# The SSD branch's sample states loaded once and turned on the chip, with the product over them cut into quarters

## The chip, the core and the metric

The kernel runs on one core of one Trainium2 chip. The metric is device time in microseconds of one execution. Five engines work side by side and are tied by semaphores: PE (TensorE, matmuls; its weight loads are listed apart as PEld), DVE (VectorE), ACT (ScalarE), POOL (GpSimd) and SP (SyncE, which here only issues DMA transfers). POOL issues DMA transfers as well.

## What is computed

The program is one inference step of a hybrid decoder layer: a prompt of 256 tokens and 8 sample sequences of 4 tokens go through the same weights. One of its branches is a Mamba-2 state-space scan (SSD) with 32 heads of 64 rows and a state of 128 columns, in 4 groups of 8 heads. For a sample sequence the state `S` comes from memory, and a chunk is its 4 tokens:

```python
    acum = jnp.cumsum(dtc * Ag, axis=1)
    ...
    y = jnp.einsum('bgrij,bjgrp->bigrp', m, xc)
    y = y + jnp.einsum('bign,bgrpn->bigrp', Cc, S) * jnp.exp(acum)[..., None]
    last = acum[:, -1]
    w = jnp.exp(last[:, None] - acum) * dtc
    S = jnp.exp(last)[..., None, None] * S + jnp.einsum('bjgr,bjgn,bjgrp->bgrpn', w, Bc, xc)
```

So each sample state is used twice: it is updated and stored (rows are head and feature, columns the state index n), and it is multiplied with C over n, for which TensorE needs n on the partitions, which is the turned layout. The second term of `y` is called the inter-chunk product below, the first one the own-token product.

## The kernel before

The weights, some 380 MB in float32, stream through SBUF once. A projection (`proj_w`) takes them in tiles of 128x512 elements (two k tiles by 256 columns): SP loads a tile (`raw`, L110, 6 buffers), ACT rounds it to the fast format (`whi`, L103), DVE computes the rest (`wlo`, L105, called the cast below), each with 5 buffers, and PE multiplies: per tile 4 matmuls on line L148, 4 on L149 and 4 on L153, of which the last 4 need the cast. All 288 tokens, prompt and sample, are the 288 moving columns. The scans of one group run inside the projections of the next: a scan is a generator, and `weave` advances it by a step for every so many tiles. After that a scheduler puts every engine's instructions in an order by its own estimate of when each can run; an engine then works strictly in its order and waits where an operand is late.

In `ssd_scan`, once per group, the state work for the samples stands at the end. Before the change, POOL loads each state twice: `load_state` brings it in rows (`sin`, 4 tiles of two sequences, tag `c4` with 6 buffers, 8 transfers of 256 KB a group), and `load_square` brings the same state in 32-column pieces of 128 bytes (`sqr`, tag `e2`, 32 transfers of 64 KB a group, two sequences ahead), so that DVE's transpose of 32x32 blocks (L941) yields the full turned matrix `st`. The updates (`updated`: one matmul on L948 and four DVE operations on L951 for a pair of heads) and the transposes (`turned`) alternate: two transposes, two updates, two transposes, two updates, for each half of the eight sequences. `inter` then does the inter-chunk product (L927: 8 matmuls with a 32-column weight `cdm`, 512 moving columns, four of them side by side in four groups of array columns) and the own-token product (L930). DVE scales and adds (L974, L977), four transposes on PE (L983) bring tokens back to columns, and DVE folds the four column groups (L985).

Of the kernel before, what the change touches and what calls it, by code (L numbers as in the profile page):

```python
# [8 lines left out]
F32 = mybir.dt.float32  # L9
# [20 lines left out]
FF = 5632  # L30
FT = FF // P
BLK = 8
NSQ = 2
RB = 6
WB = 5
STOP = object()
# [6 lines left out]
def hybrid_step(ctx: ExitStack, tc: tile.TileContext, I: dict, O: list):  # L43
# [217 lines left out]
    elcol = p1.tile([P, KT, NB], F32, name="elcol")  # L261
    scst = p1.tile([P, 24, 3 * NB + 3], F32, name="scst")
    rg = p1.tile([P, 4], F32, name="rg")
    cdm = p1.tile([P, NB, NS], F32, name="cdm")
    att = p1.tile([P, 2, P], F32, name="att")
    ats = p1.tile([P, NS], F32, name="ats")
    atsl = p1.tile([P, P], F32R, name="atsl")
    qdm = p1.tile([P, 2, NB, NS], F32, name="qdm")
    for z in (cdm, att, ats, atsl.bitcast(F32), qdm, lr3.bitcast(F32), gw3.bitcast(F32), dtbd, scst):
        G.memset(z, 0.0)  # L270
    acum_d = dram.tile([32, T], F32, name="acum_d")
    ma_d = dram.tile([P, KT, T], F32, name="ma_d")
# [7 lines left out]
    with pool("p0") as p0:  # L280
# [251 lines left out]
        def dt_prep():  # L532
            S.activation(acol, alog, ACT.Exp)
            S.activation(dte, dtx, ACT.Abs)
            S.activation(dte, dte, ACT.Exp, scale=-1.0)
            S.activation(dte, dte, ACT.Ln, bias=1.0)
            yield
            V.scalar_tensor_tensor(dtT, dtx, 0.0, dte, ALU.max, ALU.add)
            V.tensor_scalar(dte, dtT, acol, -1.0, ALU.mult, ALU.mult)
            V.tensor_tensor_scan(acumT, rm_s, dte, 0.0, ALU.mult, ALU.add)  # L540
            nc.sync.dma_start(out=acum_d, in_=acumT)

            srep = p0.tile([32, 2, 4, NS], F32, name="srep")
            V.tensor_copy(srep[:, 0], dtT[:, SEQ:T].unsqueeze(1).to_broadcast([32, 4, NS]))
            V.tensor_copy(srep[:, 1], acumT[:, SEQ:T].unsqueeze(1).to_broadcast([32, 4, NS]))
            sel = p0.tile([P, P], F32, name="sel")
            V.memset(sel, 0.0)
            G.affine_select(sel, sel, pattern=[[0, P]], compare_op=ALU.not_equal, fill=1.0, base=127, channel_multiplier=-1)
            sels = p0.tile([NS, 4, NB, NL], F32, name="sels")
            V.memset(sels, 0.0)  # L550
            G.affine_select(sels, sels, pattern=[[0, 4], [4, NB], [0, NL]], compare_op=ALU.not_equal, fill=1.0, base=3,
                            channel_multiplier=-1)
            elT = p0.tile([32, NB], F32, name="elT")
            S.activation(elT, acumT[:, SEQ:T].rearrange("p (b l) -> p b l", l=NL)[:, :, NL - 1], ACT.Exp)

# [12 lines left out]
            for i in range(3):  # L568
                for w, src in ((0, dtT), (1, acumT)):
                    s_ = src[:, i * P:(i + 1) * P] if i < 2 else srep[:, w].rearrange("p r t -> p (r t)")  # L570
                    TR(a[:, i * 64 + w * 32:i * 64 + w * 32 + 32], s_, ident[0:32, 0:32])
            V.tensor_copy(tokc.rearrange("p c x -> p (c x)"), a[:, 0:192])

            for r in range(4):
                q = slice(r * NS, (r + 1) * NS)
                V.tensor_copy(dtbd[q].rearrange("p (a r) -> p r a", r=4)[:, r],
                              tokc[q, 2, 0:32].rearrange("p (a r) -> p r a", r=4)[:, r])
                V.tensor_copy(acs[q], tokc[q, 2, 32:64].rearrange("p (a r) -> p r a", r=4)[:, r])
            yield
            yield  # L580
            a = mm_tile()
            MM(a[:, 0:32], sel, tokc[:, 0, 32:64], start=True, stop=True)
            MM(a[:, 32:64], sel, tokc[:, 1, 32:64], start=True, stop=True)
            MM(a[:, 64:96], sels.rearrange("p r b l -> p (r b l)"), tokc[0:NS, 2, 32:64], start=True, stop=True)
            V.tensor_tensor(wtok[:, 0:3, :], a[:, 0:96].rearrange("p (c x) -> p c x", x=32), tokc[:, :, 32:64], ALU.subtract)
            V.tensor_copy(wtok[:, 3, :], a[:, 32:64])
            S.activation(wtok, wtok, ACT.Exp)
            S.activation(eas, tokc[:, 2, 32:64], ACT.Exp)
            V.tensor_tensor(wtok[:, 0:3, :], wtok[:, 0:3, :], tokc[:, :, 0:32], ALU.mult)
            V.tensor_tensor(wtok[:, 3, :], wtok[:, 3, :], wtok[:, 0, :], ALU.mult)  # L590
            yield
            a = mm_tile()
            MM(a[:, 0:KT * NB], hsel.rearrange("p e x -> p (e x)"), elm.rearrange("p t b -> p (t b)"), start=True, stop=True)
            V.tensor_copy(elcol.rearrange("p t b -> p (t b)"), a[:, 0:KT * NB])

        weave(mem_proj(I["w_cv"], 2, o_pmv), dt_prep(), KT, 8)
        run(mem_proj(I["w_ck"], 3, o_pmk), mem_proj(I["w_cv"], 3, o_pmv))
# [145 lines left out]
    def ssd_scan(g, xsT, sz):  # L743
# [23 lines left out]
                    in_=I["state_ssd"][2 * q + e, h0:h0 + 8].rearrange("(t e) x n -> (e x) t n", e=2)))  # L767
            sins.append(sin)

        sqs = []  # L770

        def load_square(b):

            sq_ = e2("sqr").rearrange("p a t -> p (a t)")[:, 0:512]
            rows = I["state_ssd"][b, h0:h0 + 8].rearrange("h (y p) (g d) -> g p (h y) d", p=32, d=32)
            for i in range(4):
                tc.keep_in_program_order(G.dma_start(
                    out=sq_[32 * i:32 * i + 32].rearrange("p (r d) -> p r d", d=32), in_=rows[i]))
            sqs.append(sq_)


        bsr = rep4(bT[:, SEQ:T].unsqueeze(1), "bsr")
        yield
        a = mm_tile()
# [62 lines left out]
        for u in range(3):  # L847
# [47 lines left out]
            if u == 1:  # L895
                xsr = rep4(xsT[:, :, SEQ:T], "xsr")
            yield
        for b in range(NSQ):
            load_square(b)
        load_state(0)  # L900
        load_state(1)

        diag(cdm, cT[:, SEQ:T])
        for r in range(2):
            S.activation(mss[:, r, :], mab[:, r, :], ACT.Relu, scale=-1.0, bias=acs[:, 2 * g + r:2 * g + r + 1])
        S.activation(mss, mss, ACT.Exp, scale=-1.0)
# [5 lines left out]
        yield  # L912
        wst = r2("wst")
        stack_l(wst, wxs)
        yield


# [3 lines left out]
        def inter():  # L921
            ysi.append(la_tile())
            ysa.append(mm_tile())
            for q in (1, 0):
                for j in (3, 2, 1, 0):
                    tc.keep_in_program_order(
                        MM(ysi[0][NS * j:NS * j + NS, :], cdm[:, 4 * q + j, :], sts[4 * q + j], start=(q == 1), stop=(q == 0)))  # L927
            for r in range(2):
                tc.keep_in_program_order(
                    MM(ysa[0][NS * r:NS * r + NS, 256 * r:256 * r + 256], mss[:, r, :], xds[:, 256 * r:256 * r + 256],  # L930
                       start=True, stop=True))

        for hf_ in range(2):
            bblk = r2("bblk").rearrange("p (b n) -> p b n", n=P)
# [3 lines left out]

            def turned(b):
                st = b2("st")  # L940
                V.transpose(st, sqs[b])  # L941
                if b + NSQ < NB:
                    load_square(b + NSQ)
                sts.append(st)

            def updated(t):
# [12 lines left out]

            for x in range(4):  # L960
                turned(4 * hf_ + x)
                yield 1.5
                if x % 2 == 0:
                    continue
                for t in ((0, 1) if x == 1 else (2, 3)):
                    updated(t)
                    if hf_ == 0 and t < 2:
                        load_state(2 + t)
                    yield 1.5
        inter()  # L970
        yield
        yield
        ys = b2("ys")
        V.tensor_tensor(heads(ys), heads(ysi[0]), hb(eas[:, h0:h0 + 8], P), ALU.mult)  # L974
        for r in range(2):
            q, c = slice(NS * r, NS * r + NS), slice(256 * r, 256 * r + 256)
            V.tensor_tensor(ys[q, c], ys[q, c], ysa[0][q, c], ALU.add)  # L977
        us = b2("us").rearrange("p (t l) -> p t l", l=P)[:, :, 0:NS]
        V.tensor_tensor(us, xsT[:, :, SEQ:T], dcol[:, 4 * g:4 * g + 4].unsqueeze(2).to_broadcast([P, 4, NS]), ALU.mult)
        yield  # L980
        a = mm_tile()
        for t in range(4):
            TR(a[:, t * P:(t + 1) * P], ys[:, t * P:(t + 1) * P], ident)  # L983
        yt = pa.tile([P, P], F32, tag="cst", bufs=2, name="yt").rearrange("p (t l) -> p t l", l=NS)
        V.tensor_reduce(yt, a.rearrange("p (t j l) -> p t l j", j=4, l=NS), axis=AX.X, op=ALU.add)  # L985
        V.tensor_tensor(us, us, yt, ALU.add)
        V.tensor_tensor(sz[:, :, SEQ:T], us, sz[:, :, SEQ:T], ALU.mult)
        yield

# [997 lines left out]
```

## Time and profile before

| | |
|---|---|
| three runs | 2484.82, 2481.40, 2478.98 us, median 2481.4 |
| profiled execution | 2484.3 us, of which the span of the profile is 2482.6 |
| busy in the span | PE 99%, PEld 96%, DVE 72%, ACT 55%, POOL 18% |
| mean granted TensorE clock | 0.998 |
| DMA | 530.77 MB, mean 214 GB/s |
| the four SSD state stages | the second load of the states begins at 303, 404, 518 and 599 us; the first stage ends at 366, the last at 693 us |

A share of the span is a mean over stages. The idle time that a row gives is that of its engine just before the instruction, with what ended it. A matmul's listed duration includes its way through the pipeline; its pace is the distance between two starts.

### The profile page before, as it was taken

What the parts mean: (1) busy time and instruction counts of PE and PEld (TensorE: products, weight loads), DVE (VectorE), ACT (ScalarE), POOL (GpSimd) and SP (SyncE); (2) the same over time, 40 slices, a digit from 0 to 9 for tenths busy, and PEclk for the clock granted to TensorE, in tenths of its full rate; (3) what the DMA queues carried; (4) which work ended last, traced back from release to release, by engine and by line L of the source; (5) the groups of instructions that cost most, each with busy time, mean ns of one, the idle gap of its engine ahead of it and who ended that gap; (6) DMA issues with size and microseconds to landing.
All of it is one profiled execution on the core that took longest, in us unless ns stands there. A gap on an engine that the chain in (4) does not pass through costs nothing.

```text
span 2482.6 us, 52113 instructions
## 1 busy us (share of the span) xinstructions
PE 2466.2 (99%) x18738; PEld 2388.1 (96%) x18738; DVE 1775.2 (72%) x3804; ACT 1355.8 (55%) x2781; POOL 439.2 (18%) x798
## 2 busy tenths in 40 slices
PE   9999999999999999999999999999999999999998
PEld 8889999999999999999999989999999999999998
DVE  6866778896777766777666577667777676676766
ACT  6766647646464655554455545455555454554545
POOL 3102144143111010110111122402111001020012
PEclk9999999999999999999999999999999999999999
DMA  8877697787768686777778599655555555555555
GB/s 261 263 234 208 165 267 217 208 246 223 223 211 287 207 255 194 240 246 229 224 230 266 182 353 327 196 164 171 170 171 172 171 171 173 170 172 168 170 173 170
DMA packets 457652, 530.77 MB, mean 214 GB/s; under 512 B 40316, under 2 KB 403676, under 8 KB 457360
## 3 DMA queue, kind: packets, MB, share of 16 engines
q1 hardware_dynamic: 420272, 422.39, 56.6%
q0 software_dynamic: 37088, 105.03, 13.2%
q8 instruction: 147, 2.41, 0.4%
q14 instruction: 113, 0.93, 0.1%
q10 hardware_dynamic: 32, 0.01, 0.0%
HBM read 476.41 MB, written 50.86 MB: 212 GB/s over the span
## 4 chain that ended last, share of the span: by engine, by line
PE 96%; DMA 1%; DVE 1%; issue 0%; ACT 0%; SPq 0%; POOL 0%; DVEq 0%; ACTq 0%; POOLq 0%
PE acc L149 28%; PE acc L148 27%; PE acc L153 27%; PE acc L348 2%; PE acc L352 2%; PE acc L349 2%; PE mm L1263 1%; PE la L1254 1%; PE la L1606 1%; DMA kc<-in_cache_mem_k_dram 1%; PE mm L1218 0%; DMA raw<-in_w_ssd_out_dram 0%; PE la L1664 0%; PE la L927 0%; PE mm L948 0%
## 5 line engine op out<-in xcount | busy, mean ns | idle before, releaser
L103 ACT CAST whi<-raw 128x512 fp32r<-128x512 f32 x1464 | 898.1, 618 | 951.5 <-PE acc L149 786.1
L105 DVE TENSOR_TENSOR wlo<-raw,whi 128x512 fp32r<-128x512 f32 x1464 | 995.4, 686 | 534.3 <-ACT whi L103 527.0
L149 PE MATMUL acc<-xn,whi 128*128 128x288 f32 (+1 forms) x1936 | 541.6, 295 | 0.0
L148 PE MATMUL acc<-xn,whi 128*128 128x288 f32 (+1 forms) x1936 | 540.1, 294 | 0.3 <-ACT whi L103 0.3
L153 PE MATMUL acc<-xn,wlo 128*128 128x288 f32 (+1 forms) x1936 | 409.0, 293 | 0.0
L149 PE MATMUL acc<-hf,whi 128*128 128x288 f32 x1408 | 393.3, 296 | 0.0
L148 PE MATMUL acc<-hf,whi 128*128 128x288 f32 x1408 | 388.6, 292 | 0.0
L148 PEld LDWEIGHTS acc<-xn,whi 128*128 128x128 f32 (+1 forms) x1936 | 363.4, 188 | 4.9 <-issue 3.1
L149 PEld LDWEIGHTS acc<-xn,whi 128*128 128x128 f32 (+1 forms) x1936 | 363.7, 188 | 3.6 <-issue 0.4
L153 PEld LDWEIGHTS acc<-xn,wlo 128*128 128x128 f32 (+1 forms) x1936 | 310.4, 188 | 0.8 <-issue 0.4
L153 PE MATMUL acc<-hf,wlo 128*128 128x288 f32 x1408 | 294.5, 290 | 0.0
L149 PEld LDWEIGHTS acc<-hf,whi 128*128 128x128 f32 x1408 | 264.5, 188 | 0.0
L148 PEld LDWEIGHTS acc<-hf,whi 128*128 128x128 f32 x1408 | 264.0, 188 | 0.0
L153 PEld LDWEIGHTS acc<-hf,wlo 128*128 128x128 f32 x1408 | 226.4, 188 | 0.1
L149 PE MATMUL acc<-pr,whi 128*128 128x288 f32 x704 | 196.6, 295 | 0.0
L148 PE MATMUL acc<-pr,whi 128*128 128x288 f32 x704 | 194.8, 293 | 0.0
L1780 POOL COPY fsp<-fst 128x16 f32<-128x16 f32 x88 | 38.5, 440 | 651.8 <-DVE av L1792 433.4
L153 PE MATMUL acc<-pr,wlo 128*128 128x288 f32 x704 | 147.3, 290 | 0.0
L148 PE MATMUL acc<-un,whi 128*128 128x288 f32 x512 | 143.7, 296 | 3.3 <-ACT vT L1044 2.4
L149 PE MATMUL acc<-un,whi 128*128 128x288 f32 x512 | 143.7, 296 | 0.0
L149 PEld LDWEIGHTS acc<-pr,whi 128*128 128x128 f32 x704 | 132.3, 188 | 0.0
L148 PEld LDWEIGHTS acc<-pr,whi 128*128 128x128 f32 x704 | 132.0, 188 | 0.0
(564 smaller groups left out, 4318.4 us busy)
## 6 DMA issues: line engine op xcount, KB each, us to landing
raw<-in_w_in_dram SPq DMA_DIRECT2D x480, 256.0 KB
raw<-in_w_up_dram SPq DMA_DIRECT2D x352, 256.0 KB
raw<-in_w_down_dram SPq DMA_DIRECT2D x176, 256.0 KB
raw<-in_w_ck_dram SPq DMA_DIRECT2D x64, 256.0 KB
raw<-in_w_cv_dram SPq DMA_DIRECT2D x64, 256.0 KB
raw<-in_w_ssd_out_dram SPq DMA_DIRECT2D x64, 256.0 KB
sin<-in_state_gla_dram POOLq DMA_DIRECT2D x32, 512.0 KB, 6.4
out_dram<-sin SPq DMA_DIRECT2D x32, 512.0 KB
```

The costliest lines, as they stand in the source:

```text
L103: S.copy(hi, raw)
L105: V.tensor_tensor(lo, raw, hi, ALU.subtract)
L148: MM(a, hi[:, k, cs], xh, start=(k0 + s0 + k == 0), stop=False)
L149: MM(a, hi[:, k, cs], xl, start=False, stop=False)
L153: MM(a, lo[:, k, cs], xh, start=False, stop=(k0 + s0 + k == nk - 1))
L348: MM(accs[m], mn_hi[:, kk, ms_], hi[:, 0, :], start=(kk == 0), stop=False)
L349: MM(accs[m], mn_lo[:, kk, ms_], hi[:, 0, :], start=False, stop=False)
L352: MM(accs[m], mn_hi[:, kk, ms_], lo[:, 0, :], start=False, stop=(kk == KT - 1))
L1254: MM(osa[NS * j:NS * j + NS, :], qdm[:, k, b, :], sins[b][:, k, :], start=False, stop=(q == 1 and k == 0))
L1263: MM(a, kb[:, k * P:(k + 1) * P], vst, start=True, stop=True)
L1606: MM(ssc[NS * c:NS * c + NS, 0:P], xq[:, j, u, :], kt[:, j], start=(j == 0), stop=(j == 15))
L1780: G.tensor_copy(sp[:, :, 0:2], st.rearrange("p (b k) -> p b k", k=2))
```

## The change

The states are no longer loaded a second time. DVE transposes the rows that `load_state` brought. Because a 32x32 block transpose of rows leaves, in each block of 32 partitions, the state columns of one quarter, the product over n is cut in quarters: a weight `cdx` holds C for one quarter of n in one block of rows and zeros elsewhere, and 32 matmuls with 128 moving columns replace the 8 with 512. Their sums stand by token, block and quarter, and 16 small products with pieces of the identity (a 32-column weight, 32 moving columns) bring them to feature rows. The decays come in a matching layout (`easx`) from two products per program. The own-token product is taken with x as the weight, so that it comes out in feature rows at once. `cdx` is allocated per group in tag `c4` and is zeroed by POOL and filled by 16 small DVE copies. The transposes of a half now stand ahead of all its updates.

```diff
+            esel = p0.tile([NS, 2, P], F32, name="esel")
...
+            for e in range(2):
+                MM(a[:, 0:16], esel[:, e, :], eas[0:NS].rearrange("p (c e) -> p e c", e=2)[:, e], start=(e == 0), stop=(e == 1))
+            V.tensor_copy(easx, a[:, 0:16])
...
-        def load_square(b):
-
-            sq_ = e2("sqr").rearrange("p a t -> p (a t)")[:, 0:512]
-            rows = I["state_ssd"][b, h0:h0 + 8].rearrange("h (y p) (g d) -> g p (h y) d", p=32, d=32)
-            for i in range(4):
-                tc.keep_in_program_order(G.dma_start(
-                    out=sq_[32 * i:32 * i + 32].rearrange("p (r d) -> p r d", d=32), in_=rows[i]))
-            sqs.append(sq_)
...
-        for b in range(NSQ):
-            load_square(b)
         load_state(0)
         load_state(1)
 
-        diag(cdm, cT[:, SEQ:T])
+        cdx = c4([P, NB, 4, NS], "cdx")
+        G.memset(cdx, 0.0)
...
+        for y in range(4):
+            own_ = cdx[32 * y:32 * y + 32].rearrange("p b f (q u l) -> p f u b q l", q=2, u=4)[:, :, y]
+            for f in range(4):
+                base = own_[:, f]
+                V.tensor_copy(
+                    bass.AP(base.tensor, base.offset, [list(base.ap[0]), [4 * P + 16, 2], [P, 4], [1, NL]]),
+                    cT[32 * f:32 * f + 32, SEQ:T].rearrange("p (q j l) -> p q j l", q=2, j=4))
...
             for q in (1, 0):
-                for j in (3, 2, 1, 0):
-                    tc.keep_in_program_order(
-                        MM(ysi[0][NS * j:NS * j + NS, :], cdm[:, 4 * q + j, :], sts[4 * q + j], start=(q == 1), stop=(q == 0)))
-            for r in range(2):
+                for f in range(4):
+                    for j in (3, 2, 1, 0):
+                        b = 4 * q + j
+                        tc.keep_in_program_order(
+                            MM(ysi[0][NS * j:NS * j + NS, 0:P], cdx[:, b, f, :],
+                               sts[b].rearrange("p (t f x) -> p f t x", f=4, x=32)[:, f],
+                               start=(q == 1 and f == 0), stop=(q == 0 and f == 3)))
+            for t in range(4):
                 tc.keep_in_program_order(
-                    MM(ysa[0][NS * r:NS * r + NS, 256 * r:256 * r + 256], mss[:, r, :], xds[:, 256 * r:256 * r + 256],
-                       start=True, stop=True))
+                    MM(ysa[0][:, t * NS:t * NS + NS], xds[:, t * P:(t + 1) * P], mss[:, t // 2, :], start=True, stop=True))
...
             def turned(b):
                 st = b2("st")
-                V.transpose(st, sqs[b])
-                if b + NSQ < NB:
-                    load_square(b + NSQ)
+                V.transpose(st, sins[b // 2][:, b % 2, :])
                 sts.append(st)
...
             for x in range(4):
                 turned(4 * hf_ + x)
+                if hf_ == 0 and x % 2:
+                    load_state(2 + x // 2)
                 yield 1.5
-                if x % 2 == 0:
-                    continue
-                for t in ((0, 1) if x == 1 else (2, 3)):
-                    updated(t)
-                    if hf_ == 0 and t < 2:
-                        load_state(2 + t)
-                    yield 1.5
+            for t in range(4):
+                updated(t)
+                yield 1.5
...
-        ys = b2("ys")
-        V.tensor_tensor(heads(ys), heads(ysi[0]), hb(eas[:, h0:h0 + 8], P), ALU.mult)
-        for r in range(2):
-            q, c = slice(NS * r, NS * r + NS), slice(256 * r, 256 * r + 256)
-            V.tensor_tensor(ys[q, c], ys[q, c], ysa[0][q, c], ALU.add)
+        ys = b2("ys")[:, 0:P]
+        V.tensor_tensor(ys.rearrange("p (t x) -> p t x", x=32), ysi[0][:, 0:P].rearrange("p (t x) -> p t x", x=32),
+                        easx[:, 4 * g:4 * g + 4].unsqueeze(2).to_broadcast([P, 4, 32]), ALU.mult)
...
+        V.tensor_tensor(us, us, ysa[0][:, 0:P].rearrange("p (t l) -> p t l", l=NS), ALU.add)
         yield
         a = mm_tile()
         for t in range(4):
-            TR(a[:, t * P:(t + 1) * P], ys[:, t * P:(t + 1) * P], ident)
-        yt = pa.tile([P, P], F32, tag="cst", bufs=2, name="yt").rearrange("p (t l) -> p t l", l=NS)
-        V.tensor_reduce(yt, a.rearrange("p (t j l) -> p t l j", j=4, l=NS), axis=AX.X, op=ALU.add)
-        V.tensor_tensor(us, us, yt, ALU.add)
+            for y in (3, 2, 1, 0):
+                MM(a[32 * y:32 * y + 32, t * NS:(t + 1) * NS], ys[:, 32 * t:32 * t + 32],
+                   ident.rearrange("p (j q u l) -> p u q j l", j=4, q=2, u=4)[:, y], start=True, stop=True)
+        V.tensor_tensor(us, us, a[:, 0:P].rearrange("p (t l) -> p t l", l=NS), ALU.add)
```

The scheduler also moves instructions. Three places show how; line numbers of the changed kernel differ by a few (its casts are on L104, its transposes on L949, its state loads on L776).

PE, the end of the first group's scan, where the inter-chunk and the own-token product stand between the matmuls of a projection. Before:

```order
L149 MATMUL acc<-xn_133,whi 128x288
L148 MATMUL acc<-xn_133,whi 128x288
L927 MATMUL la<-st,cdm 32x512 x8
L930 MATMUL mm<-xds,mss 32x256 x2
L149 MATMUL acc<-xn_133,whi 128x288
```

In the change:

```order
L148 MATMUL acc<-xn_132,whi 128x288
L152 MATMUL acc<-xn_132,wlo 128x288 x2
L934 MATMUL la<-st,cdx 32x128 x32
L939 MATMUL mm<-mss,xds 128x32 x4
L147 MATMUL acc<-xn_132,whi 128x288
L148 MATMUL acc<-xn_132,whi 128x288
```

Ten matmuls have become 36, at the same place between tiles; the four transposes of L983 further on have become the 16 products of L987.

DVE, the fourth group, from behind one cast (`wlo`) on (`th`, `sz`: the prompt's outputs; `xds`, `wxs`: the sample inputs; `st`: a turned state; `ma`: evacuation of the output projection). Before:

```order
L890 SCALAR_TENSOR_TENSOR th<-xsT,dcol,mm 128x256 x2
L909 TENSOR_TENSOR xds<-mm,dtbd 128x512
L911 TENSOR_TENSOR wxs<-mm,wtok 128x512
L892 TENSOR_TENSOR sz<-th,sz 128x256
L941 STREAM_TRANSPOSE st<-sqr 128x512 x4
L892 TENSOR_TENSOR sz<-th,sz 128x256
L941 STREAM_TRANSPOSE st<-sqr 128x512
L1034 TENSOR_TENSOR ma<-acc,ma 128x288 x2
L935 TENSOR_TENSOR bblk<-bst,bmask 128x512 x2
L105 TENSOR_TENSOR wlo<-raw,whi 128x512
L706 TENSOR_TENSOR wst<-wxs,wst 64x512
L105 TENSOR_TENSOR wlo<-raw,whi 128x512
```

In the change:

```order
L889 SCALAR_TENSOR_TENSOR th<-xsT,dcol,mm 128x256 x2
L907 TENSOR_TENSOR xds<-mm,dtbd 128x512
L909 TENSOR_TENSOR wxs<-mm,wtok 128x512
L891 TENSOR_TENSOR sz<-th,sz 128x256
L949 STREAM_TRANSPOSE st<-sin 128x512 x4
L891 TENSOR_TENSOR sz<-th,sz 128x256
L949 STREAM_TRANSPOSE st<-sin 128x512 x3
L1037 TENSOR_TENSOR ma<-acc,ma 128x288
L949 STREAM_TRANSPOSE st<-sin 128x512
L1037 TENSOR_TENSOR ma<-acc,ma 128x288
L943 TENSOR_TENSOR bblk<-bst,bmask 128x512
L104 TENSOR_TENSOR wlo<-raw,whi 128x512
```

All eight transposes now stand ahead of the next cast, where five stood; the other three were spread among the casts and updates behind it.

POOL, the same group (`v_d`: the next branch's values written out, which waits for ACT). Before:

```order
L765 DMA sin<-in_state_ssd_dram 128x4x128 x4
L777 DMA sqr<-in_state_ssd_dram 32x16x32 x8
L765 DMA sin<-in_state_ssd_dram 128x4x128 x4
L777 DMA sqr<-in_state_ssd_dram 32x16x32 x8
L615 DMA v_d_8848<-vT 128x4x256
L777 DMA sqr<-in_state_ssd_dram 32x16x32 x8
```

In the change:

```order
L776 DMA sin<-in_state_ssd_dram 128x4x128 x4
L901 MEMSET cdx 128x1024
L776 DMA sin<-in_state_ssd_dram 128x4x128 x2
L626 DMA v_d_8880<-vT 128x4x256
L776 DMA sin<-in_state_ssd_dram 128x4x128 x2
L1058 DMA gw<-in_w_gla_gate_dram 16x256 x3
```

The pieces of 64 KB are gone, a memset has come in, and the last two state loads, which the last two transposes now read, stand behind `v_d`.

More of the change, by code (lines that the diff above doesn't have):

```diff
@@ L32 @@
 BLK = 8
-NSQ = 2
 RB = 6
@@ L263, in hybrid_step @@
     rg = p1.tile([P, 4], F32, name="rg")
-    cdm = p1.tile([P, NB, NS], F32, name="cdm")
+    easx = p1.tile([P, 16], F32, name="easx")
     att = p1.tile([P, 2, P], F32, name="att")
@@ L268, in hybrid_step @@
     qdm = p1.tile([P, 2, NB, NS], F32, name="qdm")
-    for z in (cdm, att, ats, atsl.bitcast(F32), qdm, lr3.bitcast(F32), gw3.bitcast(F32), dtbd, scst):
+    for z in (att, ats, atsl.bitcast(F32), qdm, lr3.bitcast(F32), gw3.bitcast(F32), dtbd, scst):
         G.memset(z, 0.0)
@@ L588, in dt_prep @@
             S.activation(eas, tokc[:, 2, 32:64], ACT.Exp)
+            esel = p0.tile([NS, 2, P], F32, name="esel")
+            V.memset(esel, 0.0)
+            for e in range(2):
+                for y in range(2):
+                    V.tensor_copy(
+                        esel[:, e].rearrange("k (j q u l) -> k u q j l", j=4, q=2, u=4)[:, 2 * e + y],
+                        ident[0:NS, 0:NS].rearrange("k (q j l) -> k q j l", q=2, j=4))
             V.tensor_tensor(wtok[:, 0:3, :], wtok[:, 0:3, :], tokc[:, :, 0:32], ALU.mult)
@@ L594, in dt_prep @@
             V.tensor_copy(elcol.rearrange("p t b -> p (t b)"), a[:, 0:KT * NB])
+            yield
+            a = mm_tile()
+            for e in range(2):
+                MM(a[:, 0:16], esel[:, e, :], eas[0:NS].rearrange("p (c e) -> p e c", e=2)[:, e], start=(e == 0), stop=(e == 1))
+            V.tensor_copy(easx, a[:, 0:16])
         weave(mem_proj(I["w_cv"], 2, o_pmv), dt_prep(), KT, 8)
@@ L768, in load_state @@
             sins.append(sin)
-        sqs = []
-        def load_square(b):
-            sq_ = e2("sqr").rearrange("p a t -> p (a t)")[:, 0:512]
-            rows = I["state_ssd"][b, h0:h0 + 8].rearrange("h (y p) (g d) -> g p (h y) d", p=32, d=32)
-            for i in range(4):
-                tc.keep_in_program_order(G.dma_start(
-                    out=sq_[32 * i:32 * i + 32].rearrange("p (r d) -> p r d", d=32), in_=rows[i]))
-            sqs.append(sq_)
         bsr = rep4(bT[:, SEQ:T].unsqueeze(1), "bsr")
@@ L914, in ssd_scan @@
         stack_l(wst, wxs)
+        for y in range(4):
+            own_ = cdx[32 * y:32 * y + 32].rearrange("p b f (q u l) -> p f u b q l", q=2, u=4)[:, :, y]
+            for f in range(4):
+                base = own_[:, f]
+                V.tensor_copy(
+                    bass.AP(base.tensor, base.offset, [list(base.ap[0]), [4 * P + 16, 2], [P, 4], [1, NL]]),
+                    cT[32 * f:32 * f + 32, SEQ:T].rearrange("p (q j l) -> p q j l", q=2, j=4))
         yield
```

## The prediction

> **What bounds the kernel now.** I read the page's busy table, its chain and its costliest groups first.
>
> ```profile
> span 2482.6 us, 52113 instructions
> PE 2466.2 (99%) x18738; PEld 2388.1 (96%) x18738; DVE 1775.2 (72%) x3804; ACT 1355.8 (55%) x2781; POOL 439.2 (18%) x798
> PE 96%; DMA 1%; DVE 1%; issue 0%; ACT 0%; SPq 0%; POOL 0%; DVEq 0%; ACTq 0%; POOLq 0%
> L103 ACT CAST whi<-raw 128x512 fp32r<-128x512 f32 x1464 | 898.1, 618 | 951.5 <-PE acc L149 786.1
> L105 DVE TENSOR_TENSOR wlo<-raw,whi 128x512 fp32r<-128x512 f32 x1464 | 995.4, 686 | 534.3 <-ACT whi L103 527.0
> ```
>
> TensorE is busy nearly everywhere, 96% of the chain is its own work, and what the weight pipeline (ACT, then DVE) waits for most is PE giving buffers back. So PE's own instructions count in full, and anything else counts only where it starves PE. The change removes 8.4 MB of transfers (128 of 64 KB), which are worth nothing on such a chain unless PE lacks data somewhere. Next, therefore, PE's waits in the four SSD stages. Only the fourth has any to speak of: one (count behind the sum, in us) for DVE, and one of 2.35 us that is shown below. Its windows:
>
> ```profile
> PE acc L148 <- DVE ma L1034: 1.0, 1, 1.0
> ```
> ```profile
> 602.00:612.00 10.00, 9.69 (x76) 9.46 (x75) 9.94 (x22) 8.30 (x19) 4.61 (x7) 1.00 0.74 195
> 612.00:622.00 10.00, 9.15 (x71) 8.92 (x69) 2.75 (x5) 2.16 (x4) 6.16 (x10) 1.00 1.06 306
> 622.00:632.00 10.00, 8.50 (x74) 8.00 (x76) 6.93 (x14) 4.01 (x7) 3.37 (x5) 0.83 0.91 255
> 632.00:642.00 10.00, 9.02 (x73) 8.65 (x70) 9.54 (x19) 3.08 (x6) 2.62 (x5) 1.00 0.29 83
> ```
>
> The columns are busy time of PE, PEld, DVE, ACT, POOL, then granted clock, DMA share, GB/s. The stage starts with DVE full (9.94 of 10). Weight buffers are freed by DVE's casts, so loads fall behind; then DMA is full (1.06) while DVE and ACT idle, and PE stands still. The clock falls after that:
>
> ```profile
> 622.00:624.00 2.00, 0.50 (x3) 0.50 (x4) 0.69 (x1) 0.92 (x2) 0.26 (x1) 0.96 1.08 277
> 624.00:626.00 2.00, 2.00 (x10) 2.00 (x9) 1.02 (x2) 1.24 (x2) 1.65 (x3) 0.50 0.67 160
> 626.00:628.00 2.00, 2.00 (x15) 1.83 (x15) 2.00 (x6) 1.16 (x2) 1.47 (x3) 0.68 0.96 332
> ```
> ```profile
> 622.53 0.62 ACT L103 CAST whi<-raw 128x512 fp32r<-128x512 f32 x1 [3.21 <-DMA raw<-in_w_ssd_out_dram]
> 623.50 0.40 PE L148 MATMUL acc<-un,whi 128*128 128x288 f32 x1 [2.35 <-ACT vT L1044]
> ```
>
> The real releaser of the 2.35 us is the weight tile that ACT waited 3.21 us for. At the lower clock another 2.00 x (0.04 + 0.50 + 0.32) = 1.7 us go. This one wait costs 4.1 us.
>
> **The change part by part.** First, PE's products. The first group's end, the narrow products and a 32-column product in rows of PE and PEld:
>
> ```profile
> 358.34 0.29 PE L148 MATMUL acc<-xn,whi 128*128 128x288 f32 x1
> 358.56 1.92 PE L927 MATMUL la<-st,cdm 128*32 128x512 f32 x16
> 360.31 0.60 PE L930 MATMUL mm<-xds,mss 128*32 128x256 f32 x4
> 360.85 0.40 PE L149 MATMUL acc<-xn,whi 128*128 128x288 f32 x1
> ...
> 364.51 0.60 PE L983 MATMUL mm<-ident,ys 128*128 128x128 f32 x4
> 364.87 0.38 PE L148 MATMUL acc<-xn,whi 128*128 128x288 f32 x1
> ```
> ```profile
> 358.56 0.64 PE L927 MATMUL la<-st,cdm 128*32 128x512 f32 x4
> ```
> ```profile
> 302.42 0.20 PEld L878 LDWEIGHTS mm<-m,xdt 128*64 128x64 f32 x4 [0.16 <-issue]
> ...
> 303.46 0.25 PEld L882 LDWEIGHTS mm<-ea,wx 128*64 128x64 f32 x4
> ```
> ```profile
> 712.77 0.53 PEld L1147 LDWEIGHTS mm<-qe,ker 128*128 128x128 f32 x4
> ```
>
> - Inter-chunk product: each float32 matmul is two passes, so 8 were 16, four side by side, 1.75 us (358.56 to 360.31). Now 64 passes of a quarter of the columns, in 16 rounds of four. L878 to L882 do rounds of 128 columns, two side by side: 302.42 to 303.46 is five times two rounds, 0.104 each; 16 x 0.104 = 1.7. Change 0. If four weight loads can't hide below so short a round, their 0.13 would pace it: +0.4.
> - Own-token product: 0.54 us (360.31 to 360.85) before. Now 8 passes with a full 128-column weight and 32 moving columns: L1147's four take (0.53 - 0.19) / 3 = 0.113 apart, 0.19 being one load's duration there; 0.90 in all, +0.36. At the narrow products' pace of a quarter round it would be -0.3.
> - Fold: four transposes took 0.36 us (364.51 to 364.87). Now 32 passes of 32 columns. Four neighbouring starts of L927 lie within 0.64 - 0.59 = 0.05 us, 0.016 apart: 0.5 us, and about 0.25 to enter and leave the column groups (0.16 idle ahead of L878 and as much behind): +0.4. Bounds: streaming alone, 8 x 0.104 / 4 = 0.2 with no such loss, -0.2; a full load's pace per side-by-side round with the loss, 8 x 0.113 + 0.25, +0.8.
>
> A rule speaks against the fold: the Trainium skill, "TensorE: Matmul & The Clock Gate", section "Wait — 56ns, not 53.3ns?", says that starts of matmuls lie at least about 25 ns apart however few columns they have. The row has 16 ns between column groups; by the rule the fold would be an estimated 0.8 us, 0.3 a group more, and the total 1.2 us more.
>
> Together 0.76 a group, 3.0 for four; the `easx` products add four loads of 0.113 once: **+3.5**, bounds -2 and +7.
>
> Second, the removed loads. The DMA view of 612 to 622:
>
> ```profile
> q1 hardware_dynamic: 1576, 1.52, 56.6%
> q0 software_dynamic: 553, 1.53, 48.7%
> ...
> sin<-in_state_ssd_dram POOLq DMA_DIRECT2D x2, 256.0 KB, 8.1
> sqr<-in_state_ssd_dram POOLq DMA_DIRECT2D x8, 64.0 KB, 6.9
> ```
>
> While weights are late, state loads take as much of the DMA engines as weights do, 8 of 64 KB among them. A tile of 0.26 MB per 12 matmuls of 0.13 us asks for 1.7 MB in 10 us, and 1.52 come. Without `sqr` they should come in time: **-4.1**, bounds -5.1 (the 0.98 us wait too) and 0.
>
> Third, the order on DVE, which the diff hides. Rows of steps back to back, and of narrow or single ones:
>
> ```profile
> 638.80 1.27 DVE L935 TENSOR_TENSOR bblk<-bst,bmask 128x512 fp32r<-128x512 f32 x2
> 642.03 0.82 DVE L1034 TENSOR_TENSOR ma<-acc,ma 128x288 f32<-128x288 f32 x2
> 645.29 2.14 DVE L951 SCALAR_TENSOR_TENSOR sin<-sin,elcol,mm 128x128 f32<-128x128 f32 x8
> ```
> ```profile
> L672 DVE SCALAR_TENSOR_TENSOR cva<-cv,scw,cva 128x312 f32<-128x312 f32 x72 | 38.8, 539 | 2.7 <-ACT cva L667 1.9
> L941 DVE STREAM_TRANSPOSE st<-sqr 128x512 f32<-128x512 f32 x32 | 22.1, 699 | 0.0
> L892 DVE TENSOR_TENSOR sz<-th,sz 128x256 f32<-128x256 f32 x16 | 6.5, 413 | 0.1
> L1585 DVE COPY xqm<-qsm 32x32 f32<-32x32 f32 x32 | 5.5, 172 | 0.6
> ```
>
> Neighbours overlap by about 0.085 us: 512 columns cost 0.60, 288 cost 0.36, an update 0.26, a copy of 32x32 0.09. DVE can be five casts ahead of PE, no more. I count, in the order, from a cast that had to wait for PE to the cast at which PE is tightest, DVE's work against PE's. Third group, change: 10 casts, 8 transposes, 5 more of that width (23 x 0.60 = 13.8), 9 `ma` (3.2), 8 updates (2.1), 3 `cva` (1.4), 9 of `th`, `sz`, `xsT` (about 0.33 each, 2.9), 16 copies into `cdx` (1.5): 24.9. PE has 154 tile matmuls x 0.13 (19.9), four updates of 0.22, 12 narrow products (1.3), five transposes (0.6): 22.7. DVE is **2.2 short**. Counted so, the old order had 1.7 to spare there (14.2 against 15.9). Fourth group: 19.5 against 18.3, 1.2 short; the old order had 0.4 to spare (21.0 against 21.4) and still the 0.98 wait, so real waits run 1.4 beyond the count. First and second group: 0.1 and 0.8 to spare; old, over 3. The cause is the bunch of transposes and copies, which nothing hides once five casts are used up. By the bare count 2.2 + 1.2 = 3.4 us, with 1.4 on each group 2.2 + 1.2 + 1.3 + 0.6 + 2.8 = 8.1; less the old 0.98, 2.4 to 7.1: **+4.7**. Below nothing is excluded only if the count is too high by 2 us; then it is -1.
>
> POOL loses 32 issues a group and gains one memset, behind which the last four state loads stand; GLA, attention and FFN don't change.
>
> Sum: 3.5 - 4.1 + 4.7 = **+4.1** on the profiled execution's 2484.3, which lies 2.9 above the median; from the median, **2485.5 us**.
>
> **The rivals.**
>
> - *Transposes wait for their state at DVE's head* (slower). The eight stand almost together, and the last pair's load waits for one of six `c4` buffers (two `m`, four `sin`, now `cdx`: seven) and in the fourth group for `v_d`. Casts queue behind. For it: a state took 8.1 us to land in that window. Against it: 4.9 is the median of all 32 (row below), and traffic falls. It decides once the last load is later than the transposes ahead of it, 6 x 0.60 us. At 8.1 - 4.9 = 3.2 in three groups it costs 9.6, and one fall of the clock 1.7: +15, 2497.
> - *Weights late anyway*: what starts the trouble is DVE without casts, and the bunch makes that longer; then the 4.1 stay. +8, 2490.
> - *The count is too high and PE cheap*: DVE isn't short, products cost 0: -5, 2476. For it: the order moves casts' matmuls back, which gives PE other work. Against: two groups are short.
>
> ```profile
> sin<-in_state_ssd_dram POOLq DMA_DIRECT2D x32, 256.0 KB, 4.9
> ```
>
> **How the numbers follow.** Forecast 0.45, own range 2480 to 2489; first rival 0.15, second 0.17, third 0.23 (two of the three terms reach further down than up). About 0.2% (5 us) is what can be told here from no change, so within is 2476.4 to 2486.4. The forecast, whose middle lies just below that bound, gives 0.29 to the same, 0.13 to slower and 0.03 to faster; the first rival all to slower; the second 0.06 to the same and 0.11 to slower; the third, whose middle lies at the lower bound, 0.09 to the same and 0.14 to faster. Faster 0.17, same 0.44, slower 0.39. The range goes from just below the third rival to just short of the first: 2475 to 2496.
>
> **What would show it.** L927's successor keeps its 1.7 us; the own-token product takes 0.9, the fold 0.75. The 3.2 us wait of ACT for weights near 622 and the 0.50 clock are gone. PE shows new waits on DVE's casts in the third and fourth group, under 1.5 us each, and none on a state load. Wrong: DVE waiting for `sin` (first rival), ACT for weights in that stage (second), or no PE wait at all there (third).

## The result and the profile after

| | median | runs |
|---|---|---|
| before | 2480.49 us | 2478.98 to 2484.82, 4 runs |
| changed | 2507.01 us | 2506.8 to 2507.44, 4 runs |
| ratio | 1.0104 | 95% interval 1.0087 to 1.0122 |

The change costs 26.5 us, where the prediction had +4 and 2496 as its upper end. The first rows of the page of the changed kernel, its span, its busy engines and its chain:

```profile
span 2505.5 us, 52604 instructions
PE 2483.7 (99%) x19062; PEld 2404.4 (96%) x19062; DVE 1781.1 (71%) x3862; ACT 1356.2 (54%) x2781; POOL 357.3 (14%) x673
PE 95%; DVE 3%; DMA 1%; issue 0%; ACT 0%; SPq 0%; DVEq 0%; ACTq 0%
```

DVE's share of the chain has gone from 1% to 3%, which is where a forecast of waits would look. But the span has grown by 22.9 us, and of that PE's *busy* time by 17.5 (2483.7 against 2466.2), of which the sum had 3.5. So most of the loss is no wait at all, which is the first thing that the prediction did not provide for. PE's waits (who was waited for: sum, times, longest, in us):

```profile
PE acc L147 <- DVE ma L1037: 5.7, 2, 3.6
PE mm L1150 <- DVE qe L1098: 1.6, 1, 1.6
PE mm L954 <- DVE bblk L943: 1.5, 1, 1.5
...
PE acc L152 <- DVE wlo L104: 0.7, 1, 0.7
PE mm L954 <- DVE wst L717: 0.5, 1, 0.5
```

The wait near 623 us is gone. PE waits for DVE instead, 8.4 us of it in the state stages (the 1.6 lies at 1088 us). Here is the largest, in the third group, in the timelines of PE and DVE (start, length, what it is, and in brackets the idle time before it):

```profile
547.88 0.69 PE L152 MATMUL acc<-un,wlo 128*128 128x288 f32 x4
552.18 0.37 PE L147 MATMUL acc<-un,whi 128*128 128x288 f32 x1 [3.61 <-DVE ma L1037]
```
```profile
538.00 1.09 DVE L917 COPY cdx<-bc 32x32 f32<-32x32 f32 x6
...
550.22 0.70 DVE L949 STREAM_TRANSPOSE st<-sin 128x512 f32<-128x512 f32 x1
550.85 0.82 DVE L957 SCALAR_TENSOR_TENSOR sin<-sin,elcol,mm 128x128 f32<-128x128 f32 x3
551.58 0.82 DVE L1037 TENSOR_TENSOR ma<-acc,ma 128x288 f32<-128x288 f32 x2
```

DVE never pauses there; the `ma` that frees PE's accumulator stands behind transposes and updates. The clock falls after the wait (a window; the clock is the third number from the right):

```profile
555.00:557.00 2.00, 2.00 (x10) 2.00 (x10) 2.00 (x4) 1.00 (x2) 0.00 (x0) 0.50 0.71 206
```

That is the mechanism that was forecast, but it does not reach 26 us. The rest shows where nothing was changed. The stretch from 160 to 190 us holds only the projections of the memory, 1220 to 1280 us only a projection on `xn`, and 1310 to 1380 us only the one on `mx`, with their weights. PE's windows there (busy us and matmuls, clock, DMA share, GB/s), before and after:

```profile
160.00:190.00 30.00, 30.00 (x135) 1.00 0.73 229
1220.00:1280.00 60.00, 60.00 (x464) 1.00 0.75 236
1310.00:1380.00 70.00, 70.00 (x541) 1.00 0.76 241
```
```profile
160.00:190.00 30.00, 30.00 (x130) 1.00 0.67 213
1220.00:1280.00 60.00, 60.00 (x458) 1.00 0.79 249
1310.00:1380.00 70.00, 70.00 (x534) 1.00 0.83 264
```

PE is busy throughout at full clock and does fewer of the same matmuls. From the distances of their starts: in the first 200 us 0.227 us became 0.233 for 512 columns, and near 1350 us six matmuls (half a weight tile) take 0.790 us instead of 0.780.

A place could explain that. `easx` (64 bytes a partition) took the slot of `cdm` (1024 bytes), so all tiles allocated behind it lie 960 bytes lower: `mn_hi`, the operand of the first 200 us, moved from byte 120832 to 119872, `un`, the operand of the output projections, from 215808 to 214848. By 256 both had remainder 0 and have 64 now. `xn`, `mx`, `whi` and `wlo` did not move.

### The profile page after: what moved, and what is told of

It is laid out like the page before. It is cut to its first block, busy times and chain, and to the rows that moved or that the text cites. A ratio compares the mean times of both kernels' runs of the same rounds, so it can differ in the third digit from the quotient of the medians.

```text
span 2505.5 us, 52604 instructions
## 1 busy us (share of the span) xinstructions
PE 2483.7 (99%) x19062; PEld 2404.4 (96%) x19062; DVE 1781.1 (71%) x3862; ACT 1356.2 (54%) x2781; POOL 357.3 (14%) x673
## 4 chain that ended last, share of the span: by engine, by line
PE 95%; DVE 3%; DMA 1%; issue 0%; ACT 0%; SPq 0%; DVEq 0%; ACTq 0%
PE acc L148 27%; PE acc L147 27%; PE acc L152 27%; PE acc L347 2%; PE acc L348 2%; PE acc L351 2%; PE mm L1266 1%; PE la L1257 1%; PE la L1609 1%; PE la L1667 1%; DVE wlo L104 1%; DVE st L949 1%; PE mm L1221 0%; DMA raw<-in_w_in_dram 0%; PE la L934 0%
## 5 line engine op out<-in xcount | busy, mean ns | idle before, releaser
L104 DVE TENSOR_TENSOR wlo<-raw,whi 128x512 fp32r<-128x512 f32 x1464 | 994.5, 686 | 553.0 <-ACT whi L102 543.1
```

The lines of the kernel that those rows point to most:

```text
L104: V.tensor_tensor(lo, raw, hi, ALU.subtract)
```

## The experiments

First, the old kernel alone is shifted, by 64 and by 128 bytes, and the changed one is brought from remainder 64 to 128. No instruction moves on any engine in any of the three; for 128 bytes the 16 below is 32.

```diff
-    cdm = p1.tile([P, NB, NS], F32, name="cdm")
+    cdm = p1.tile([P, NB * NS + 16], F32, name="cdm")[:, 0:NB * NS].rearrange("p (b s) -> p b s", b=NB)
```
```diff
-    easx = p1.tile([P, 16], F32, name="easx")
+    easx = p1.tile([P, 32], F32, name="easx")[:, 0:16]
```

> The kernel before with 64 bytes of padding behind the tile cdm: every engine's instructions and their order are those of before, only tiles allocated later lie 64 bytes further, as they do (modulo 128) in the changed kernel. Theory A (place): the changed kernel loses part of its 26 us because its tiles are no longer on multiples of 128 bytes; in its first 200 us, where the change adds almost nothing, it is 6 us behind and the 512-column matmuls start 0.231 to 0.236 us apart instead of 0.227. By A this kernel loses the same: 6 us by 200 us and some 15 us in all, near 2496. Theory B (the change's own work): the new products and the bunch on DVE cost it all; then this kernel is the one before, 2480 to 2484, with starts 0.227 apart.

> The same with 128 bytes of padding. Theory A says that what counts is the remainder by 128, so 2480 to 2484 and starts 0.227 us apart. If any new place of the tiles disturbed (theory A in a weaker form), it would lose as much as with 64 bytes. By B again 2480 to 2484.

> The changed kernel with easx allocated 128 bytes wide instead of 64, of which the same 64 are used: instructions and order are those of the changed kernel, tiles allocated later lie on the same remainder by 128 as before. Theory A: the 6 us of the first 200 us come back and the slower tile periods behind 700 us (1.58 to 1.61 us instead of 1.56) too, in all some 15 us: near 2492. What is left against the kernel before is then the change's own, mostly the waits of PE for DVE. Theory B: 2507.

Measured: the old kernel 64 bytes further 2506.29 us, ratio to before 1.0098 (1.0083 to 1.0113); 128 bytes further 2491.99, 1.0042 (1.0027 to 1.0057); the changed kernel at 128 bytes 2502.97, 1.0086 (1.0069 to 1.0103). Each set of runs had runs of the kernel before beside it, with medians from 2480.49 to 2482.68 us; the ratios go by these, and differences between kernels of two sets are good to some 2 us. So 64 unused bytes make the old kernel as slow as the change does, and theory B is out as the whole cause. The remainder by 128 is not the rule: at 128 both are still slow, if less. PE's windows of the old kernel at +64 and at +128:

```profile
160.00:190.00 30.00, 30.00 (x130) 1.00 0.66 220
1310.00:1380.00 70.00, 70.00 (x534) 1.00 0.84 268
```
```profile
160.00:190.00 30.00, 30.00 (x131) 1.00 0.69 219
1310.00:1380.00 70.00, 70.00 (x533) 1.00 0.79 254
```

The 24 us of the first are not pace alone: of the 20.4 us between the two profiled executions, 8.7 arise between 539 and 653 us, where it has waits and two falls of the clock that the change doesn't have, so that it comes to the same time as the change is in part chance. Two of its waits, and a window in the first of the falls:

```profile
PE acc L148 <- ACT whi L103: 3.6, 3, 3.1
PE acc L148 <- ACT vT L1044: 2.9, 2, 1.9
```
```profile
566.00:572.00 6.00, 5.71 (x23) 5.61 (x24) 3.88 (x9) 2.10 (x4) 0.72 (x1) 0.50 1.03 326
```

Next, the changed kernel at the old remainder by 256 (seven small tiles of the first pool aside); the same with its transposes spread; and in the old kernel the two suspected operands moved one at a time, each with the tiles behind it in its pool.

```diff
-    easx = p1.tile([P, 16], F32, name="easx")
+    easx = p1.tile([P, 64], F32, name="easx")[:, 0:16]
-        mrs = p0.tile([P, 2], F32, name="mrs")
+        mrs_ = p0.tile([P, 8], F32, name="mrs"); mrs = mrs_[:, 0:2]
-        acol = p0.tile([32, 1], F32, name="acol")
+        acol = mrs_[0:32, 2:3]
-            hpar = p0.tile([32, 2], F32, name="hpar")
+            hpar = mrs_[0:32, 3:5]
```

> The changed kernel, instructions and order kept, with easx allocated 256 bytes wide and two tiny tiles put inside another, so that every tile behind has the same remainder by 256 bytes as in the kernel before (768 bytes lower). Theory A (place, by the remainder by 256): the 512-column matmuls of the first 200 us go back to 0.227 us apart, the periods behind 1150 us to 1.56 us, and what is left against the kernel before is the change's own: PE's waits for DVE (10.5 us here, with a fall of the clock of some 1.7) and its products (some 3 us), less the 5 us that the kernel before loses near 624 us: near 2490. Theory A2 (any other place than that of the kernel before disturbs): near 2503, as with 128 bytes.

Measured: 2493.85 us, 1.0051 (1.0036 to 1.0066). Of the 26.5 us, 13.2 (2507.01 - 2493.85) are place. The profiled executions of the two bear it out: the changed kernel falls behind by 5.2 us up to 222 us and by 8.8 between 665 and 1400 us, and not in the state stages between. The windows are those of the kernel before again:

```profile
160.00:190.00 30.00, 30.00 (x134) 1.00 0.67 224
1220.00:1280.00 60.00, 60.00 (x464) 1.00 0.78 241
1310.00:1380.00 70.00, 70.00 (x541) 1.00 0.81 258
```

The waits for DVE are those of the changed kernel, and the clock falls twice:

```profile
PE acc L147 <- DVE ma L1037: 6.0, 3, 3.6
PE mm L954 <- DVE bblk L943: 1.5, 1, 1.5
...
PE acc L152 <- DVE wlo L104: 0.7, 1, 0.7
PE mm L954 <- DVE wst L717: 0.5, 1, 0.5
```
```profile
547.00:551.00 4.00, 4.00 (x21) 4.00 (x20) 4.00 (x11) 0.54 (x1) 0.00 (x0) 0.57 0.37 111
649.00:653.00 4.00, 4.00 (x21) 4.00 (x21) 3.94 (x8) 0.62 (x1) 1.21 (x3) 0.59 0.23 65
```

By the windows, 4 x (0.43 + 0.41) = 3.4 us go at the lower clock; with the 8.7 of waits, 12.1 us.

An update overwrites the state that a transpose reads, so the four transposes of a half have to precede its updates; but those of the second half can stand between the updates of the first (the four DVE operations of an update are held in program order in the same way):

```diff
-                V.transpose(st, sins[b // 2][:, b % 2, :])
+                tc.keep_in_program_order(V.transpose(st, sins[b // 2][:, b % 2, :]))
...
             for x in range(4):
-                turned(4 * hf_ + x)
-                if hf_ == 0 and x % 2:
+                if hf_ == 1:
+                    break
+                turned(x)
+                if x % 2:
                     load_state(2 + x // 2)
                 yield 1.5
             for t in range(4):
                 updated(t)
                 yield 1.5
+                if hf_ == 0:
+                    turned(4 + t)
+                    yield 1.5
```

> The kernel of the run before (same remainders by 256) with the transposes of the second four sequences put between the updates of the first four, and DVE's transposes and updates held in that order: nothing is added or removed. Theory C: PE's waits for DVE in the third and fourth group come from the bunch of eight transposes. Then they go, from 10.5 us to under 2, the fall of the clock with them, and the time is some 9 us under the run before: near 2481. If the waits come from DVE's work as a whole in those groups (the copies into cdx, the evacuations of the output projection), they stay and the time with them.

Measured: 2483.73 us, 1.0010 (1.0001 to 1.0020), 10.1 us below the run before. The waits for DVE fall from 8.7 to 2.6 us, not to under 2, and the clock falls nowhere before the end. Theory C holds for most of them; 2.6 us stay:

```profile
PE acc L147 <- DVE ma L1042: 2.2, 3, 1.5
...
PE acc L152 <- DVE wlo L104: 0.4, 1, 0.4
```

The two operands:

```diff
-        mn_hi = p0.tile([P, KT, SEQ], F32R, name="mn_hi")
+        mn_hi = p0.tile([P, 16 + KT * SEQ], F32R, name="mn_hi")[:, 16:].rearrange("p (k t) -> p k t", t=SEQ)
```
```diff
-        un = pa.tile([P, 8, T], F32R, tag="un", bufs=1, name="un")
+        un = pa.tile([P, 16 + 8 * T], F32R, tag="un", bufs=1, name="un")[:, 16:].rearrange("p (k t) -> p k t", t=T)
```

> The kernel before, with 64 bytes of padding ahead of mn_hi in the pool of the first 200 us alone: mn_hi, mn_lo and the other tiles of that pool lie 64 bytes further, all later tiles where they were; instructions and order are the same. Theory A, by operand: the 512-column matmuls, which read mn_hi and mn_lo, run 0.233 apart instead of 0.227, some 900 of them: +6 us at 200 us, and then nothing more, 2487. If it is not these operands that make the first 200 us slow: 2481.

> The kernel before, with un (the operand of the output projections) and four small tiles behind it 64 bytes further; instructions, order and the first 200 us are the same. By operand: half a weight tile on un takes 0.798 us instead of 0.780, 256 of them: +4.6 us, 2486, and the projections on xn keep their pace. Theory P (PE keeps a slower pace, once it has fallen into it, until something breaks its rhythm): the projection on xn and mx from 1200 to 1400 us, whose operands have not moved, stays at 0.790 for half a tile instead of 0.780 behind the last output projection, 267 half tiles: +2.7 us more, and the like in earlier stretches: 2489 or above.

Measured: with `mn_hi` moved 2486.13 us, 1.0020 (1.0011 to 1.0029); with `un` moved 2488.35, 1.0026 (1.0016 to 1.0036). PE's windows of the two kernels:

```profile
160.00:190.00 30.00, 30.00 (x130) 1.00 0.63 215
...
1310.00:1380.00 70.00, 70.00 (x541) 1.00 0.77 246
```
```profile
160.00:190.00 30.00, 30.00 (x134) 1.00 0.68 229
1220.00:1280.00 60.00, 60.00 (x458) 1.00 0.72 228
1310.00:1380.00 70.00, 70.00 (x534) 1.00 0.77 248
```

Each operand slows its own part, and together they cost 11.0 us against the 2481.76 of the kernel before in their set (4.4 and 6.6), most of the 13.2. With `mn_hi` moved the first 200 us are slow (0.233) and the late stretch is not. With `un` moved it is the other way round, and more: 1220 to 1280 us is the projection on `xn`, 1310 to 1380 on `mx`, neither of which was moved, and both lost pace. From the starts: `xn` near 0.780 for half a tile just before 1157 us, then `un` at 0.800, and behind it `xn` and `mx` at 0.790 for 267 halves on end. The time alone, between the 2486 and the 2489 that were expected, would not have decided it.

That fits a pace that PE keeps once it was brought into it. Three single matmuls between tiles of that projection test this, in this kernel and in the old one:

```diff
+        if j2 in (1, 3, 5):
+            mids.append([0, lambda: tc.keep_in_program_order(
+                MM(mm_tile()[:, 0:T], ones.bitcast(F32R), mx(0)[0], start=True, stop=True))])
         run(proj(I["w_mix_out"], 256 * j2, 256, mx, KT, cons))
```

> The kernel before with un 64 bytes further, as measured, and three single extra matmuls (ones times a part of mx, result unused) between weight tiles of the projection on mx, in its second, fourth and sixth block of 16 tiles; nothing else. Theory P (a rhythm of PE that holds until it is broken): the projection, which ran its half tiles at 0.790 us from the last output projection to its end, leaves that pace at one of the three breaks and goes to 0.780, or to some other pace that then holds again; at least one break changes it. If the pace of 0.790 comes from where something lies, or from other work of that stretch, it is 0.790 between and behind the breaks too.

> The kernel before with the same three extra matmuls. Theory P: its pace of 0.780 us for half a tile may be lost at a break; if it is, the slower pace holds up to the next break. If pace comes from the place of the operands: 0.780 throughout, with three steps of some 0.13 us.

One run each: 2488.4 us with `un` moved, 2482.65 for the old kernel. In the first the pace is 0.790 before, between and behind the three, so the expectation that at least one of them would change it was not met. The old kernel's windows without and with the extra matmuls (the last stretch lies behind all three, 40 us each):

```profile
1345.00:1385.00 40.00, 40.00 (x310) 1.00 0.70 220
```
```profile
1220.00:1280.00 60.00, 60.00 (x463) 1.00 0.77 239
...
1350.00:1390.00 40.00, 40.00 (x306) 1.00 0.64 205
```

It had 0.780 up to the first extra matmul and 0.790 from there to the end of the projection, through the other two. One matmul put in between costs 0.13 us, and then some 1% of what follows. So this run shows that the pace of 0.780 can be lost without moving anything, and that the slower one is then kept. What decides which pace is taken, and what ends the slower one, is not shown.

Last, the two other terms of the sum. The old loads are put back with the old function (into tiles that nobody reads), and, in another kernel, the copies into `cdx` are taken off DVE; both on the spread version.

```diff
+        def load_square(b):
...
+        for b in range(2):
+            load_square(b)
         load_state(0)
...
                 tc.keep_in_program_order(V.transpose(st, sins[b // 2][:, b % 2, :]))
+                if b + 2 < NB:
+                    load_square(b + 2)
```
```diff
-                V.tensor_copy(
+                G.tensor_copy(
                     bass.AP(base.tensor, base.offset, [list(base.ap[0]), [4 * P + 16, 2], [P, 4], [1, NL]]),
```

> The changed kernel at the old remainders with its transposes spread (2483.7 us measured), and with the 32 loads of 64 KB a group of the kernel before issued again by POOL, at the places in the program where they stood; nobody reads what they bring. It tells what the removed loads were worth. Prediction's theory (they made the weights late near 620 us, 4.1 us with the fall of the clock): ACT waits for weights again in the fourth group, PE with it, +4 us, near 2488. If the removed loads were worth nothing there (the start of that stage alone did it, or DVE hid it): 2484.

> The same kernel (2483.7 us), without those loads, and with the 16 small copies into cdx done by POOL instead of DVE. DVE then has 16 x 0.09 = 1.4 us a group less, and its order in the third and fourth group is nearly that of the kernel before. If what is left of PE's waits for DVE (2.6 us) comes from that work: -2 us, near 2481.5, level with the kernel before or just below. If POOL's copies make the last state loads late, which stand behind them in its queue, DVE waits for sin and it is slower than 2484.

With the loads 2485.24 us, 1.0015 (1.0006 to 1.0024), 1.5 above the spread version, and the intervals overlap. DMA is full again in the fourth group, ACT does not wait for weights there, and PE does not stop:

```profile
605.00:615.00 10.00, 10.00 (x82) 10.00 (x81) 8.58 (x18) 6.87 (x15) 6.78 (x11) 1.00 1.03 266
615.00:625.00 10.00, 10.00 (x80) 10.00 (x79) 7.62 (x23) 4.42 (x8) 3.43 (x7) 1.00 1.08 287
```

A full DMA alone does not make the wait of 2.35 us, then. What else it needed is not shown; the order in which POOL issues these loads is not quite the old one, since nobody reads them.

With the copies on POOL 2479.05 us, 0.9991 (0.9982 to 1.0001), 4.7 below the spread version. In the state stages PE has no wait left; DVE never waits for a state there. Of the 4.8 us between the two profiled executions 4.0 arise between 531 and 545 us, where the spread version has its four waits. They cost more than the 2.6 us listed, since a listed wait begins only at the end of the matmul ahead, whose 0.29 us are longer than its pace of 0.13. Against the kernel before this is level or a little faster, and it is the best form of the change that was run; against the change as it was, 28 us.

## Why the prediction was wrong

The sum had three terms and one assumption that it did not write down: that PE's other matmuls keep their pace.

- **PE's products, +3.5.** Right in kind and a little too high, in the fold. After, first group:

```profile
357.15 1.95 PE L934 MATMUL la<-st,cdx 128*32 128x128 f32 x64
359.03 1.08 PE L939 MATMUL mm<-mss,xds 128*128 128x32 f32 x8
359.94 0.38 PE L147 MATMUL acc<-xn,whi 128*128 128x288 f32 x1
...
364.50 0.43 PE L152 MATMUL acc<-xn,wlo 128*128 128x288 f32 x2
364.86 0.46 PE L987 MATMUL mm<-ident,ys 128*32 128x32 f32 x32
365.25 0.40 PE L147 MATMUL acc<-xn,whi 128*128 128x288 f32 x1
```

  Inter-chunk 1.88 (forecast 1.75), own-token 0.91 (0.90). The fold takes 0.39 from its first start to the next matmul, and its first start comes 0.09 later behind the matmul before than that of the old transposes, 0.48 in all (0.75). Together that is 0.63 a group more than before, against 0.76. What was over-priced is the distance of the fold's starts: its 32 products start within 0.26 us, not 0.5. The prediction took 0.59 from a row of 0.64 whose four products last 0.617 each; the starts lie 0.007 apart and not 0.016, and in the fold rounds of four follow each other after 0.032. The Trainium skill's floor of about 25 ns between starts ("TensorE: Matmul & The Clock Gate", section "Wait — 56ns, not 53.3ns?") does not hold for products side by side in column groups: it would have made 0.8 us.
- **The removed loads, -4.1.** The wait and its fall of the clock did go, as forecast. But the loads alone are not its price: put back they cost 1.5 us, and the intervals overlap. And the 4.1 was the price in one execution, of 2484.3 us, which the sum took off the median of 2481.4. The old kernel with the three extra matmuls is the kernel before up to 1293 us; in its execution the same stage has these waits, and the clock does not fall:

```profile
PE acc L148 <- DVE ma L1034: 1.5, 1, 1.5
PE acc L148 <- ACT vT L1044: 1.0, 1, 1.0
```
```profile
624.00:630.00 6.00, 6.00 (x71) 5.34 (x69) 5.40 (x12) 2.48 (x4) 2.58 (x4) 1.00 1.03 301
```

- **The order on DVE, +4.7 (bounds -1 to +7.1).** The mechanism was right (the third and fourth group, casts and `ma` behind the bunch, no wait for a state), the size was not. In place of 4.7 it measured 10.1 for the bunch (6.1 us of waits and 3.4 at the lower clock) and 4.7 for the copies. The waits of the changed kernel, 8.4 us in the state stages, are near the 8.1 of the count with 1.4 on each group; the forecast took the middle and subtracted the old wait. Three steps fell short. The count of the third group, 2.2 short, met 5.1 us of waits (1.5 and 3.6 above): it went by the lead of the casts, while what PE waited for were `bblk` and an `ma`, which frees an accumulator. The falls of the clock behind the long waits (3.4 us in the kernel at the old remainder) were put into the first rival and not into this term. And the copies into `cdx` were priced at 0.09 us each, as neighbours that overlap; six take 1.09 in the row of `cdx` above, 0.18 each.
- **The pace of PE**, 13.2 us, had no term. The prediction doesn't mention where tiles lie; the 960 bytes by which `easx` in the slot of `cdm` moves every later tile are in two lines of the whole diff, which the shortened one above leaves out. Between half a tile at 0.780 and at 0.790 lies 1.3%, on a kernel that is PE's own work for 96% of its chain.

The parts are +13.2 (place), +10.1 (bunch), +4.7 (copies) and -1.4 for the rest (2479.05 against 2480.49). They come to 26.5 us because each kernel is compared with the next one of a chain, so the sum confirms none of them. The rest is what the change is worth without these three: some 2.5 us of products (4 x 0.63) and a little for `easx`, less the waits that the kernel before has near 624 and 638 us (with the lower clock 5 us in the one execution, 2.5 in the other).

Of the rivals, the first (DVE waits for a state) and the second (weights late) did not happen. The third (DVE isn't short, products cost nothing) was wrong on both: DVE was short, and the products cost some 2.5 us. Of the signs that were listed, the own-token product at 0.9 us, the end of ACT's wait near 622 us and no wait on a state load came; the fold at 0.75 us, the end of the 0.50 clock (it came back near 555 us) and waits under 1.5 us each did not; PE busy for 17.5 us more, the clearest sign, was not on the list.

## What to carry to other kernels

When a change adds, drops or resizes a tile, every tile allocated behind it moves: before anything is argued about instructions, compare the remainders (here by 256 bytes) of the matmul operands, and as a test shift the old kernel by the same bytes with nothing else changed. Where PE is the bound, compare the number of matmuls in a stretch that was not touched, before reading any wait. And a bunch on an engine with 28% of its time free still stalls PE if it stands in front of what frees a buffer: order the long operations between the short urgent ones.

## What was not expected of the hardware

- The start-to-start time of matmuls depends on where an operand lies: 512 columns with `mn_hi` and `mn_lo` took 0.227 us at remainder 0 by 256 bytes, 0.232 at 128 and 0.233 at 64, the clock 1.00 in all. Half a tile on `un` took 0.798 to 0.800 in every stretch at 64 and 0.790 to 0.793 at 128; at 0 it took 0.780 in some stretches and 0.790 in others. Other remainders, and whether 256 is the whole rule, were not tried.
- PE's pace has a memory: 0.780 and 0.790 us for the same six matmuls on the same operands, each held for tens of microseconds; one extra matmul switched 0.780 to 0.790, and five others, put in at 0.790, did not switch it back.
